# Issuing the first large load of a max-pooling kernel from SyncE instead of ScalarE

## The chip, the cores and the metric

The kernel runs on one core of a Trainium2 chip. The metric is the device time of one execution in microseconds (us); lower is better. A comparison uses the median of several executions.

## The reference

The input `x` is float32 of shape 32 x 256 x 4096 (134.2 MB) and `output_size` is 256. The reference is adaptive max pooling along the last axis:

```python
for i in range(output_size):
    start = int(i * length / output_size)
    end = int((i + 1) * length / output_size)
    result[:, :, i] = np.max(x[:, :, start:end], axis=-1)
```

4096 is a multiple of 256, so every output is the maximum of W = 16 neighbouring floats (a window, 64 bytes). There are 2,097,152 windows, 16,384 for each of the 128 partitions, and the output is 8.4 MB.

## The kernel before, in words

The windows are cut into two groups, and inside a group each partition owns one contiguous run of windows. Group A is 9,340 windows for each partition and is read by ten loads: a short one of 128 windows (8 KB in each partition), eight of 1,024 windows (64 KB in each partition, 8,192 KB in all) and one of 1,020. Group B is 7,044 windows in six loads of 1,024 and a last one of 900. The sixteen loads behind the short one are called load 0 to load 15 here, by the value of `n_loads` (load 0 is the first large one, load 8 the one of 1,020, load 15 the one of 900).

All loads go into one SBUF tile, `ring`. It has two halves of 1,176 windows (`CHUNK + GAP`). Even loads use the lower half and odd ones the upper. Every second load of a half is moved up by `GAP` = 152 windows, so two loads that follow each other in one half overlap in 872 windows only. The short load lies in the lower half at windows 1,024 to 1,151.

VectorE is the only engine that computes. `pooled` (line 56) is one `reduce_max` over windows. The short load takes one of 128 windows; every large load takes two, first the 872 windows that the next load of that half will overwrite, then the other 152. Load 15 takes a single one of 900, written back into the ring. The results lie in the tile `kept`.

Order around the change. The program order of the first three loads is: short load (line 85), load 0 (line 95), load 1 (line 95). These wait for nothing. The short load and load 1 are issued by SyncE (SP in the profile) and load 0 by ScalarE (ACT), because of the line with `queue` below. All later loads are issued by SP. Load 2 overwrites windows of load 0 and of the short load, so SP issues it only when both have landed and VectorE has reduced the short load and the first 872 windows of load 0. Load k + 2 waits for load k in the same way: for its landing and for its reduce of 872. VectorE takes its reduces in program order: the short load, then load 0, load 1 and so on.

```python
queue = nc.scalar if n_loads == 0 else nc.sync
queue.dma_start(out=ring[:, at * W : (at + n) * W], in_=xn)
...
for u, v in parts if moved else parts[::-1]:
    pooled(dst[:, u:v], at + u, v - u)
```

At the end ScalarE stores the 900 results of load 15 (line 112), and SP stores the kept results of group A and of group B (line 115).

A DMA of 128 partitions is carried by 16 DMA engines, eight partitions each; the profile counts its pieces as packets, one for each partition (8 KB for the short load, 64 KB for a large one) and one small one for each engine at the end. The profile names the two issuing queues q1 (SP) and q10 (ACT).

Of the kernel before, what the change touches and what calls it, by code (L numbers as in the profile page):

```python
# [1 line left out]

# [4 lines left out]


@with_exitstack
def kernel(  # L10
    ctx: ExitStack,
    tc: tile.TileContext,
    x: bass.AP,
    output_size: bass.AP,
    out: bass.AP,
):

    nc = tc.nc
    P = nc.NUM_PARTITIONS
    fp32 = mybir.dt.float32

    B, C, L = x.shape
    O = int(output_size)  # L30
    assert L % O == 0, (L, O)
    W = L // O
    total = B * C * O // P
    assert B * C * O % P == 0

    CHUNK = 1024
    GAP = 152
    FIRST = 128
    LOADS_A, LOADS_B = 9, 6

    LESS = 4
    group_a = [FIRST] + [CHUNK] * (LOADS_A - 1) + [CHUNK - LESS]
    last = total - sum(group_a) - LOADS_B * CHUNK
    group_b = [CHUNK] * LOADS_B + [last]
    assert 0 < last and last * (W + 1) <= CHUNK * W

    pool = ctx.enter_context(tc.tile_pool(name="pool", bufs=1))
    ring = pool.tile([P, 2 * (CHUNK + GAP) * W], fp32, tag="ring", name="ring")
    kept = pool.tile([P, total - last], fp32, tag="kept", name="kept")

    xw = x.flatten_outer_dims().rearrange("r (o w) -> (r o) w", w=W)
    ow = out.flatten_outer_dims().rearrange("r o -> (r o)")

    def pooled(dst, at, n):

        nc.vector.reduce_max(  # L56
            out=dst,
            in_=ring[:, at * W : (at + n) * W].rearrange("p (n w) -> p n w", w=W),
            axis=mybir.AxisListType.X,
        )  # L60

    taken = 0

    def group(n):

        nonlocal taken
        span = slice(taken * P, (taken + n) * P)
        taken += n
        return (
            xw[span].rearrange("(p n) w -> p (n w)", p=P),  # L70
            ow[span].rearrange("(p n) -> p n", p=P),
        )

    stores = []
    n_loads = 0
    base = 0
    for g, loads in enumerate((group_a, group_b)):
        xg, og = group(sum(loads))
        a = 0
        for n in loads:  # L80
            xn = xg[:, a * W : (a + n) * W]
            dst = kept[:, base + a : base + a + n] if n != last else None
            if n == FIRST:

                nc.sync.dma_start(
                    out=ring[:, CHUNK * W : (CHUNK + n) * W], in_=xn
                )
                pooled(dst, CHUNK, n)
            else:

                low = n_loads % 2 * (CHUNK + GAP)
                moved = n_loads // 2 % 2
                at = low + moved * GAP
                queue = nc.scalar if n_loads == 0 else nc.sync
                queue.dma_start(out=ring[:, at * W : (at + n) * W], in_=xn)
                if n != last:
                    cut = CHUNK - GAP if moved else GAP
                    parts = [(0, cut), (cut, n)]
                    for u, v in parts if moved else parts[::-1]:
                        pooled(dst[:, u:v], at + u, v - u)  # L100
                else:
                    end = (at + CHUNK) * W
                    last_kept = ring[:, end - n : end]
                    pooled(last_kept, at, n)
                n_loads += 1
            a += n
        full = a - last if g else a
        stores.append((og[:, 0:full], kept[:, base : base + full]))
        base += full
    assert taken == total  # L110

    nc.scalar.dma_start(out=og[:, full : full + last], in_=last_kept)
    tc.no_sync_barrier()
    for dst, src in stores:
        nc.sync.dma_start(out=dst, in_=src)


# [1 line left out]
_INS = ['x', 'output_size']  # L119
_OUTS = [((32, 256, 256), 'float32')]  # L120

_NUMBERS = {'output_size': 256}


# [26 lines left out]
```

## Time and profile before

| | |
|---|---|
| median of 3 executions | 337.42 us (336.9 to 337.74) |
| the profiled execution's own time | 336.9 us |
| its span | 335.1 us, 1.8 us less than its own time |
| VectorE busy | 276.3 us (82%) in 32 reduces |
| DMA | 142.61 MB, mean 426 GB/s; busy share 0.9 or near it in all 40 slices |
| reduce of 872 windows / of 152 / of 128 | 14.7 us / 2.7 us / 2.3 us |
| short load, load 0, load 1: issue to landing | 24.8, 25.0 and 43.8 us |

The span is the time from the first to the last instruction of the profiled execution; its own time is what the clock of the metric gave for that execution. Times inside the span are counted from its start. "Busy share" of DMA is the mean over the 16 DMA engines; a packet is put where it starts, so in short stretches the share can go over 1. "SPq" and "ACTq" are the queues of the issuing engines: their rows tell when a DMA was issued, not when it moved data.

### The profile page before, as it was taken

The numbers are of one execution on the slowest core, as the hardware profiler recorded it, in microseconds if no ns is written. First come the engines' busy times: TensorE is split into PE (matmuls) and PEld (weight loads), VectorE is DVE, ScalarE is ACT, GpSimd is POOL, SyncE is SP. The second block draws the span as 40 slices with busy tenths as digits, with TensorE's granted clock in tenths as the row PEclk, the third lists the DMA queues.
The fourth block names the chain that finished last, engine by engine and source line by source line (L and its number), as shares of the span: only waits on it lengthen the run. The fifth ranks groups of instructions, "written<-read, shape, count | busy, mean of one in ns | idle before, by whom it ended". The sixth has DMA issues, their size and how long they took to land.

```text
span 335.1 us, 113 instructions
## 1 busy us (share of the span) xinstructions
DVE 276.3 (82%) x32; POOL 0.2 (0%) x4
## 2 busy tenths in 40 slices
DVE  0009999698897979899797979979797997979993
POOL 0000000000000000000000000000000000000000
DMA  9998999999999999989999999999898989999997
GB/s 382 454 408 383 493 368 399 446 422 446 430 422 454 407 469 391 477 383 462 413 444 430 422 454 422 454 399 477 383 493 375 501 375 462 415 455 440 391 410 310
DMA packets 2880, 142.61 MB, mean 426 GB/s; under 512 B 320, under 2 KB 320, under 8 KB 448
## 3 DMA queue, kind: packets, MB, share of 16 engines
q1 hardware_dynamic: 2592, 133.76, 92.7%
q10 hardware_dynamic: 288, 8.85, 6.2%
HBM read 134.22 MB, written 8.39 MB: 426 GB/s over the span
## 4 chain that ended last, share of the span: by engine, by line
DMA 57%; DVE 36%; DVEq 5%; issue 0%
DMA ring<-in_x_dram 57%; DVE kept L56 36%; DVEq L146 5%
## 5 line engine op out<-in xcount | busy, mean ns | idle before, releaser
L56 DVE TENSOR_REDUCE kept<-ring 128x152 f32<-128x2432 f32 (+3 forms) x31 | 261.2, 8472 | 53.7 <-DMA ring<-in_x_dram 53.7
L56 DVE TENSOR_REDUCE ring<-ring 128x900 f32<-128x14400 f32 x1 | 15.1, 15143 | 0.0
L132 POOL MEMSET const-bfloat16-1.0<- 128x1 bf16 x1 | 0.1, 101 | 0.0
L132 POOL MEMSET const-uint8-127<- 128x1 uint8 x1 | 0.1, 101 | 0.0
L132 POOL MEMSET const-float32-0.0<- 128x1 f32 x1 | 0.1, 98 | 0.2 <-issue 0.2
L132 POOL MEMSET const-float32-1.0<- 128x1 f32 x1 | 0.1, 98 | 0.0
## 6 DMA issues: line engine op xcount, KB each, us to landing
ring<-in_x_dram SPq DMA_DIRECT2D x1, 8160.0 KB, 23.9
ring<-in_x_dram SPq DMA_DIRECT2D x1, 7200.0 KB, 21.6
out_dram<-kept SPq DMA_DIRECT2D x1, 4670.0 KB, 32.4
out_dram<-kept SPq DMA_DIRECT2D x1, 3072.0 KB, 18.2
ring<-in_x_dram SPq DMA_DIRECT2D x1, 1024.0 KB, 24.8
out_dram<-ring ACTq DMA_DIRECT2D x1, 450.0 KB, 4.2
ring<-in_x_dram SPq DMA_DIRECT2D x13, 24.0
ring<-in_x_dram ACTq DMA_DIRECT2D x1, 25.0
```

The costliest lines, as they stand in the source:

```text
L56: nc.vector.reduce_max(out=dst, in_=ring[:, at * W : (at + n) * W].rearrange("p (n w) -> p n w", w=W), axis=mybir.AxisListType.X,)
L132: nc = _bacc.Bacc("TRN2", target_bir_lowering=False, num_devices=1)
L146: with _tile.TileContext(nc) as tc:
```

## The change

Load 0 is issued by SyncE instead of ScalarE. SyncE then issues the short load, load 0 and load 1 one behind the other, all on its own queue. Sizes, places in the ring, the reduces and their order, the waits and all other DMAs stay as they are; ScalarE keeps one DMA, the store of the last 900 results.

```diff
                 low = n_loads % 2 * (CHUNK + GAP)
                 moved = n_loads // 2 % 2
                 at = low + moved * GAP
-                queue = nc.scalar if n_loads == 0 else nc.sync
-                queue.dma_start(out=ring[:, at * W : (at + n) * W], in_=xn)
+                nc.sync.dma_start(out=ring[:, at * W : (at + n) * W], in_=xn)
```

Lines behind the change move up by one: line 95 of before is line 94 after it.

## The prediction

> **What bounds the kernel now.** I read the page first: its slices, then its chain.
>
> ```profile
> DVE  0009999698897979899797979979797997979993
> DMA  9998999999999999989999999999898989999997
> ...
> DMA ring<-in_x_dram 57%; DVE kept L56 36%; DVEq L146 5%
> ```
>
> Each digit covers 8.4 us. VectorE has nothing for three slices, then pauses again and again; the DMA engines never stop. The chain alternates loads and reduces, so it doesn't yet say which of the two sets the pace. The timeline of the starts of the reduces does (start, busy time, and in brackets the idle time ahead):
>
> ```profile
> 25.58 36.67 DVE L56 TENSOR_REDUCE kept<-ring 128x128 f32<-128x2048 f32 x5 [25.58 <-DMA ring<-in_x_dram]
> 65.42 17.28 DVE L56 TENSOR_REDUCE kept<-ring 128x872 f32<-128x13952 f32 x2 [3.17 <-DMA ring<-in_x_dram]
> 84.87 17.28 DVE L56 TENSOR_REDUCE kept<-ring 128x872 f32<-128x13952 f32 x2 [2.17 <-DMA ring<-in_x_dram]
> 104.23 17.28 DVE L56 TENSOR_REDUCE kept<-ring 128x872 f32<-128x13952 f32 x2 [2.09 <-DMA ring<-in_x_dram]
> ```
>
> From 84.87 to 104.23 is 19.36 us for one load, of which VectorE needs 17.28 and waits 2.1. 8.389 MB in 19.36 us are 433 GB/s. The kernel is bound by DMA, at a constant rate; a change gains only where the DMA engines stand idle or run slowly. So I looked for such places, by cutting the span at the landings (columns: length, VectorE, GpSimd, clock, DMA share, GB/s):
>
> ```profile
> 42.48:44.96 2.48, 2.48 (x1) 0.00 (x0) 1.00 1.03 370
> 44.96:65.42 20.46, 17.29 (x4) 0.00 (x0) 1.00 0.97 416
> 65.42:84.87 19.45, 17.28 (x3) 0.00 (x0) 1.00 1.00 431
> 84.87:104.23 19.36, 17.28 (x2) 0.00 (x0) 1.00 1.00 433
> ```
>
> There is one such place before the end: load 2 takes 20.46 us after load 1, and load 3 takes 19.45, where the steady value is 19.36. That is 1.10 + 0.09 = 1.19 us lost. Why it happens is seen in the chain in order of time (start, length):
>
> ```profile
> 25.58 16.89 DVE kept L56 x2
> 42.47 0.02 issue
> 42.48 22.91 DMA ring<-in_x_dram
> ...
> 80.13 24.08 DMA ring<-in_x_dram
> ```
>
> Load 2 is issued at 42.48, and load 1, the last one in the queue, lands at 44.96: a lead of 2.48 us. Load 4 is issued at 80.13 and load 3 lands at 84.85: a lead of 4.72. A lead of 4.7 keeps the DMA engines fed, one of 2.5 doesn't. The lead is short because VectorE reduces the short load (2.29) only when load 0 has landed too: 16.89 us are 2.29 of the short load, overlapping a little, and 14.68 of load 0. And the short load comes late (24.8 us from issue to landing) because its pieces take turns with load 0's on the other queue. DMA packets from 4.9 to 24 us:
>
> ```profile
> q10 hardware_dynamic: 112, 7.34, 88.6%
> q1 hardware_dynamic: 112, 0.92, 11.3%
> ```
>
> 112 pieces of 64 KB on q10, 112 of 8 KB on q1: one for one. A piece took 0.886 x 19.1 x 16 / 112 = 2.42 us and 0.113 x 19.1 x 16 / 112 = 0.308 us. The eighth 8 KB piece of an engine thus stands behind seven of 64 KB.
>
> **The change part by part.** *Order.* On one queue the eight short pieces of an engine go ahead of load 0's. They need about 8 x 0.308 = 2.5 us, and the first ones are dearer (14 packets in the first 2.3 us):
>
> ```profile
> q1 hardware_dynamic: 14, 0.11, 32.1%
> ```
>
> 0.321 x 2.3 x 16 / 14 = 0.84 us for a cold piece, 0.54 more than a warm one. No data moves before 1.7 us, so the short load should land near 1.75 + 0.84 + 7 x 0.308 = 4.8, plus some tenths for its completion: about 5 us instead of 25.55. Its reduce of 2.29 us then lies at 5 to 7.5, under load 0's transfer, which ends some 18 us later.
>
> *Load 0.* An engine moves the same eight short and eight large pieces ahead of load 0's end; only their order differs. Load 0 lands at 25.57 as before: nothing gained, nothing lost.
>
> *Load 2.* The reduce of 872 windows starts at 25.57, not 27.78, and ends at 40.25. SP issues load 2 at 40.27 instead of 42.48, 2.21 us earlier; load 1 still lands at 44.95, so the lead is 4.68, as in the steady loop. The stretch of 1.10 and its echo of 0.09 go. What is late next: nothing but the DMA rate, 19.36 a load.
>
> *The end.* Loads 2 to 15, the reduces and the stores are chained to these landings without slack that could swallow it: load 14 lands at 297.65, then 17.07 and 15.19 of reduces, the last store and its completion. All of it moves 1.19 earlier.
>
> *Issue.* ScalarE loses one DMA (0.40 us of issue at 0.73), SP gains one. Load 0's issue moves to 1.16 behind the short load's, load 1's by about 0.43 to 1.59. Cover for load 0: 0.73 + 1.0 is where the first data of the short load moved, so load 0's pieces can start at about 2.2 to 2.8, while the short load keeps every engine busy to about 4.8. Without that cover it would cost 0.43 to 1. Load 1's pieces are wanted at 24. No wait is added; nothing is queued on SP but loads 1 and 2, which are not wanted yet. ScalarE has nothing to do until line 112.
>
> *The unknown: a cold start with short pieces only.* Before, the second piece of an engine was a large one. Its first large pieces (2.3 to 4.9 us):
>
> ```profile
> q10 hardware_dynamic: 16, 1.05, 97.3%
> ```
>
> 0.973 x 2.6 x 16 / 16 = 2.53 us, 0.11 over the warm 2.42. If only the first piece is cold, whichever follows, the change saves that 0.11. If all eight short pieces cost 0.84, it costs 7 x 0.54 = 3.8 us. I take 0, near the first end: the 8 KB pieces from 4.9 on, the nearest warm rows, take 0.308, and the pieces of 64 KB follow each other without a gap.
>
> The Trainium skill speaks against the change in one place: "DMA: Bandwidth & Descriptors", section "Issuing engines are not separate DMA queues", says that DMAs from different engines run on the same 16 DMA engines, and that issuing from several saves only the time to initiate them. By that alone the change loses an issue, 0.4 us or nothing, and gains nothing. The rows above agree on the engines and the rate; what the rule leaves out is that the queue decides who lands first. The same page's section "Measured" gives a 1 MB transfer 6.15 us (issued from GpSimd); by an estimate from that figure the short load would land at about 8 us and the sum would turn to a loss near 2 us.
>
> **The sum.** -1.19 + 0 = -1.19 us. Span 335.1 - 1.19 = 333.9; its own time 336.9 - 1.19 = 335.7. The median shown is 0.52 above that execution, so I predict 337.42 - 1.19 = 336.2 us, 0.35% less. A measurement of this kernel can tell about 0.3% (1.0 us) from no change, so the forecast stands just beyond that line.
>
> **The rivals.** *1. Real gain, too small to tell (0.32).* The lead of load 2 grows, but part of the 1.19 is given back at the start: 0.43 of a later issue, or one or two more cold pieces at 0.54 each. For it: nothing in the trace shows a single queue starting alone. Time: 336.4 + 0.43 to 1.0, so 336.5 to 337.4. That nothing changes at all also falls here: the short load's early landing seems certain, its worth isn't.
>
> *2. Slower (0.14): the cold queue of short pieces.* Place: the first 8 us, where all 16 engines have only 8 KB pieces in hand. Price: up to 3.8 us, so 337.42 - 1.19 + 3.8 = 340.0; typical, half of that, 338.1. It decides from a mean of 0.308 + (1.19 + 0.54) / 8 = 0.52 us a piece. For it: 0.84 for the cold ones, and that before, a 64 KB piece lay between any two short ones. Against it: 0.308 is already 27 GB/s an engine, the rate of the large pieces.
>
> *3. More gain (0.08).* In the start, or after, the slowest engine's lag shrinks too. The first DMA stretches show different engines starting at different times (1.7 to over 2.3 us); half a microsecond of it could go: 335.6.
>
> **How the numbers follow.** The forecast has 0.46: 336.2, within 335.8 and 336.5. With rival 3 that makes 0.54 for faster by over 0.3%, rival 1 is 0.32 within, and 0.14 slower. The range takes in the forecast, rival 3 less 0.2 for the scatter of the executions (0.4 about their median), rival 1 and the lower end of rival 2: 335.3 to 338.0.
>
> **What would show it.** Right: the first reduce starts near 5 us, alone; load 0's reduce still near 25.6; load 2's issue near 40.3, and the landings from 44.95 on all 19.36 apart; the DMA share is 1.00 from 45 to 65; span near 333.9. Wrong at the start: load 0's reduce at 26.5 or later, with a first reduce at 7 or later. Wrong on the lead: load 2 is issued 4.7 ahead and still lands 20.4 after load 1. Then the lag is that of a queue and not of the lead.

## The result and the profile after

The changed kernel takes 334.87 us (334.78 to 335.01, six executions); the kernel before took 337.50 us on the same chip (336.90 to 337.74, six executions). The ratio is 0.9925, interval 0.9913 to 0.9938: 2.6 us faster. Forecast were 336.2 us and a gain of 1.19. The direction was right; the time lies 0.4 us under the range.

The profiled execution took 334.98 us, its span is 333.2 us (before 336.9 and 335.1). Its slices:

```profile
DVE  2009979797997979799797979979797998979993
DMA  9898989899898989899898989899898989899987
```

VectorE now has something to do in the first slice. The timeline of the reduces (start, busy time, idle time ahead):

```profile
5.40 2.29 DVE L56 TENSOR_REDUCE kept<-ring 128x128 f32<-128x2048 f32 x1 [5.40 <-DMA ring<-in_x_dram]
24.75 17.28 DVE L56 TENSOR_REDUCE kept<-ring 128x872 f32<-128x13952 f32 x2 [17.07 <-DMA ring<-in_x_dram]
44.13 17.28 DVE L56 TENSOR_REDUCE kept<-ring 128x872 f32<-128x13952 f32 x2 [2.10 <-DMA ring<-in_x_dram]
63.55 17.28 DVE L56 TENSOR_REDUCE kept<-ring 128x872 f32<-128x13952 f32 x2 [2.14 <-DMA ring<-in_x_dram]
```

The short load is reduced alone at 5.40. Load 0 starts its reduce at 24.75, where before nothing was reduced until 25.58. Load 1 lands at 44.11 instead of 44.94: 0.83 us came from the start, where the forecast had nothing. The span cut at the landings shows the rest:

```profile
24.75:44.12 19.37, 17.28 (x2) 0.00 (x0) 1.00 1.00 433
44.13:63.53 19.40, 17.28 (x2) 0.00 (x0) 1.00 1.00 432
63.55:82.87 19.32, 17.28 (x2) 0.00 (x0) 1.00 1.00 434
```

The stretch of 20.46 us at load 2 is gone, and its echo. In the chain, load 2 is issued at 39.47, 4.6 us ahead of load 1's landing at 44.11:

```profile
24.75 14.70 DVE kept L56
39.45 0.02 issue
39.47 24.06 DMA ring<-in_x_dram
```

So between these two profiles 0.83 us came from the start and 1.1 from load 2 and its echo, 1.9 in all. The medians differ by 2.6: the profiled execution of before was the quickest of its six. What the others lose, and how much of it is the lead's, took experiments.

### The profile page after: what moved, and what is told of

It is laid out like the page before. It is cut to its first block, busy times and chain, and to the rows that moved or that the text cites. A ratio compares the mean times of both kernels' runs of the same rounds, so it can differ in the third digit from the quotient of the medians.

```text
span 333.2 us, 113 instructions
## 1 busy us (share of the span) xinstructions
DVE 276.5 (83%) x32; POOL 0.2 (0%) x4
## 4 chain that ended last, share of the span: by engine, by line
DMA 57%; DVE 36%; DVEq 5%; issue 0%; SPq 0%
DMA ring<-in_x_dram 57%; DVE kept L56 36%; DVEq L145 5%; SPq L85 0%
```

## The experiments

"Lead" is the time from the issue of load 2 to the landing of load 1, the last one queued ahead of it. Landing times are the last of a load's sixteen completion marks in the trace, one for each DMA engine; "spread" is from the first mark to the last. These marks, and the packet records used further down, stand in the trace; no view prints them one by one. A "lag" is what a load takes beyond the steady 19.35 us. The kernel before ran beside all of these; its medians there were 337.06, 337.60, 337.47 and 337.41 us.

**The kernel before, twice more** (b_again, b_third). No edit.

> The kernel before, unchanged, profiled a second time. Theory 1 (the gain has two terms: about 0.83 us because two queues that start at once let one DMA engine begin late, and about 1.1 us because load 2 is issued only 2.5 us ahead of load 1's landing): load 0's reduce again follows a first reduce at 25.3 us or later, and load 2 lands 20.2 to 20.7 us after load 1. Theory 2 (only the lead counts, the late landing of load 0 was an accident of that one execution): the first reduce can start anywhere from 24.7 to 25.6, and the second term is the same.

> The kernel before, profiled a third time. Two profiles of it gave load 2 at 20.45 and 21.21 us behind load 1, at the same lead of 2.5 us, and their spans differ by 0.7. If it is this lag that makes its executions differ: a span s goes with a lag of load 2 and 3 together of about s - 333.9 us (1.2 at 335.1, 1.9 at 335.8), and the landing of load 1 stays within 44.5 to 45.0.

They took 337.56 and 337.43 us; their spans are 335.8 and 335.7 us. The timeline of b_again:

```profile
25.31 36.66 DVE L56 TENSOR_REDUCE kept<-ring 128x128 f32<-128x2048 f32 x5 [25.31 <-DMA ring<-in_x_dram]
65.88 17.28 DVE L56 TENSOR_REDUCE kept<-ring 128x872 f32<-128x13952 f32 x2 [3.92 <-DMA ring<-in_x_dram]
85.44 17.28 DVE L56 TENSOR_REDUCE kept<-ring 128x872 f32<-128x13952 f32 x2 [2.28 <-DMA ring<-in_x_dram]
```

The start is late again (25.31, and 25.32 in b_third against 24.75). Load 1 lands at 44.65 in both, 0.54 later than after the change. The lead is 2.4 again, but load 2 now takes 21.21 and 21.22 us after load 1, 0.8 more than in the first profile and more than the 20.7 that was expected at most. Load 2 and load 3 together lag 2.07 and 1.88 us, close to what was expected of b_third from its span (1.8). In these three profiles what differs most is the lag of load 2; load 1's landing differs by 0.29.

**Two queues, long lead** (e1_two_long). The short load moves to a place that load 2 does not overwrite, and is reduced after load 0's 872 windows; ScalarE still issues load 0.

```diff
-                    out=ring[:, CHUNK * W : (CHUNK + n) * W], in_=xn
+                    out=ring[:, SPOT * W : (SPOT + n) * W], in_=xn   # SPOT = CHUNK + GAP + CHUNK
...
+                            with tc.issue_after(first):   # load 0's 872
+                                late = pooled(*short)
...
```

> The kernel before with both queues at the start, but a long lead: the short load lies in the upper half of the ring and is reduced after the 872 windows of load 0. Theory 1: the start stays late (first reduce near 25.5 us), load 2 is issued near 40.3 and lands 19.4 us after load 1, so only the lead's term goes: 337.5 - 1.1 = 336.4 us. Theory 2 (only the lead): 334.9 us, as the changed kernel.

Measured: 335.45 us (335.25 to 335.50), ratio 0.9948 (0.9935 to 0.9960). The start is late and load 2 no longer is:

```profile
25.38 36.66 DVE L56 TENSOR_REDUCE kept<-ring 128x872 f32<-128x13952 f32 x5 [25.38 <-DMA ring<-in_x_dram]
63.91 17.28 DVE L56 TENSOR_REDUCE kept<-ring 128x872 f32<-128x13952 f32 x2 [1.88 <-DMA ring<-in_x_dram]
```

Load 1 lands at 44.54, and with a lead of 4.45 load 2 lands 19.34 behind it. The lead alone brings 1.6 us, more than the 1.1 expected, and without touching the queue. What is left to the changed kernel, some 0.4 to 0.6 us, is the late start.

**One queue, load 0 ahead of the short load** (e2_one_short).

```diff
+                if n_loads == 0:   # behind load 0's dma_start, on nc.sync
+                    xs, ds, ns = short
+                    nc.sync.dma_start(
+                        out=ring[:, CHUNK * W : (CHUNK + ns) * W], in_=xs
+                    )
+                    pooled(ds, CHUNK, ns)
```

> One queue (SP) for everything, as changed, but the short load is issued behind load 0, so that it lands with it and its 2.3 us of reduce delay load 2 again (lead about 2.4 us). Theory 1: load 0 and the short load land at 24.7 us or a little earlier, load 2 lands about 20.4 us after load 1: 334.9 + 1.1 = 336.0 us. If the lag of load 2 belongs to two queues and not to the lead: 334.9 us. If only the lead counts (theory 2): 337.5 us.

Measured: 335.44 us (335.30 to 335.68), ratio 0.9950 (0.9937 to 0.9964). This missed its aim: load 0 landed 2.5 us before the short load, VectorE took its 872 windows first, from 22.96, load 2 was issued at 39.86 and the lead was 4.9, not 2.4. There was no lag (19.34). But it shows something else: load 1 lands at 44.76, 0.65 us later than after the change, with one queue. The first packets in flight (window 0 to 2.35 us):

```profile
q1 hardware_dynamic: 16, 1.05, 135.9%
```

1.359 x 2.35 us = 3.2 us for each of the sixteen first pieces of 64 KB, against 2.42 in the steady loop. The spread of load 1's marks is 0.86 us, against 0.33 after the change. A late start doesn't need a second queue.

**A small DMA on the second queue** (e3_tiny_act), added to the changed kernel.

```diff
+                nc.scalar.dma_start(out=tiny[:, :], in_=xn[:, 0:W])
                 nc.sync.dma_start(
```

> The changed kernel plus one small DMA on ScalarE's queue at the start (64 bytes for each partition, 8 KB in all, its result unused), issued together with the short load. Theory 1 in its narrow form (two queues that are handed work in the same instant make an engine begin late, whatever the size): the short load's reduce starts near 6 us and load 0's near 25.5; 334.9 + 0.8 = 335.7 us. If it is the large pieces between the short ones that delay the start (theory 3): 334.9 to 335.1 us, load 0's reduce at 24.8.

Measured: 335.02 us (334.95 to 335.47), load 0's reduce at 24.88:

```profile
5.54 2.29 DVE L56 TENSOR_REDUCE kept<-ring 128x128 f32<-128x2048 f32 x1 [5.54 <-DMA ring<-in_x_dram]
24.88 17.28 DVE L56 TENSOR_REDUCE kept<-ring 128x872 f32<-128x13952 f32 x2 [17.05 <-DMA ring<-in_x_dram]
```

Two queues that start together cost some 0.1 us here. The narrow form of theory 1 falls.

**Two queues with small first pieces** (e7_two_small). SP issues the short load; ScalarE issues load 0, cut into 8 KB and 56 KB for each partition, and load 1.

```diff
-                nc.sync.dma_start(out=ring[:, at * W : (at + n) * W], in_=xn)
+                queue = nc.scalar if n_loads < 2 else nc.sync
+                for u, v in ((0, 128), (128, n)) if n_loads == 0 else ((0, n),):
+                    queue.dma_start(...)
```

> Two queues at the start, but only 8 KB pieces first: SP issues the short load, ScalarE issues load 0 in two DMAs (8 KB and 56 KB for each partition) and load 1 behind them. The lead is long. If large pieces among the first ones cause the late start (theory 3): load 1 lands at 44.2 or earlier, 334.9 to 335.2 us. If two queues do it (theory 1): load 1 lands at 44.5 to 44.9, 335.5 us or more.

Measured: 338.37 us, scattered from 335.86 to 339.60, and no answer on its question. The profile is of one of the quick executions (336.06). In it load 0 landed at 25.08, 0.35 later than after the change, between the two theories. Then load 2 on SP's queue took turns with the rest of load 1 on ScalarE's, so that load 1 landed at 46.85 only, load 3 was issued 2.2 us ahead of load 2's landing, and a short lead was back one load later.

**The price of the lead on one queue.** The changed kernel, with some windows of load 0 reduced once more ahead of its 872, into a place that is overwritten later (in e4 into a tile of its own). The order of the reduces behind it is fixed to that of the changed kernel.

```diff
+                    if n_loads == 0:
+                        first = pooled(spare, at + cut, EXTRA)   # EXTRA = 64, 128, 192 or 256
...
```

> The changed kernel once more, as the control for the three runs beside it: 334.9 us, load 0's reduce at 24.8, a lead of 4.6 us (issue of load 2 to the landing of load 1), load 2's reduce 19.4 us after load 1's.

> The changed kernel, with 64 windows of load 0 reduced once more ahead of its 872 (1.2 us of VectorE, result unused), so that load 2 is issued that much later: lead 3.5 us. If the lag of load 2 is a matter of the lead alone: a small loss, 0 to 0.4 us, 334.9 to 335.3. If it needs two queues at the start: 334.9 us.

> The changed kernel, with 128 windows of load 0 reduced once more ahead of its 872 (2.2 us of VectorE, result overwritten later): lead 2.4 us as in the kernel before, but on one queue. With 64 windows (lead 3.5) load 2 took 19.66 us. If the lead decides: load 2 lands 20.3 to 21.2 us after load 1, 1.0 to 2.0 us lost, 336.0 to 337.0 us. If a lag at this lead needs two queues at the start: under 335.4 us.

> The changed kernel with 192 windows reduced once more: lead about 1.35 us, between 2.42 (no lag) and 0.40 (2.0 us lag). If on one queue each us of lead below 2.4 costs one: load 2 lands 20.3 to 20.6 us after load 1, time 335.9 to 336.2 us.

> The same with 256 windows (4.3 us): lead about 0.3 us. If the lead decides and each us below about 3.5 costs one us: load 2 lands 22.5 to 23.5 us after load 1, 338.1 to 339.1 us. A loss much under 3 us would mean that something makes it good later.

| kernel | lead, us | load 2 behind load 1, us | time, us |
|---|---|---|---|
| a_again (no extra windows) | 4.6 | 19.33 | 335.15 (334.80 to 335.38) |
| e4_lead_64 | 3.5 | 19.66 | 335.04 (334.97 to 335.37) |
| e5b_lead_128 | 2.4 | 19.39 | 335.01 (334.81 to 335.11) |
| e8_lead_192 | 1.5 | 21.41 | 336.63 (336.05 to 337.12) |
| e6b_lead_256 | 0.4 | 21.35 | 337.07 (336.82 to 338.12) |

Of e5b's two branches the second came, and the theory that the lead alone decides falls: 2.4 us of lead cost the kernel before 1.2 to 2.1 us in its profiles, and cost nothing here. The 0.3 us that load 2 lags in e4 doesn't show in its times. Nor is the price a slope. From 2.4 to 1.5 the lag jumps to about 2 us (the median rises by 1.6, more than was expected of e8), and from 1.5 to 0.4 it grows no more (e6b was expected at 338.1 or more). The windows at the joint between load 1 and load 2 (length, VectorE, GpSimd, clock, DMA share, GB/s) show this. In e5b_lead_128 there is no gap:

```profile
42.50:44.50 2.00, 2.00 (x2) 0.00 (x0) 1.00 1.23 524
44.50:46.50 2.00, 2.00 (x1) 0.00 (x0) 1.00 1.21 524
```

In e6b_lead_256 no piece starts for 2 us, and in the kernel before (the last pair) fewer do:

```profile
42.50:44.50 2.00, 2.00 (x2) 0.00 (x0) 1.00 0.00 0
44.50:46.50 2.00, 2.00 (x2) 0.00 (x0) 1.00 1.55 524
```

```profile
42.50:44.50 2.00, 2.00 (x1) 0.00 (x0) 1.00 0.84 295
44.50:46.50 2.00, 2.00 (x2) 0.00 (x0) 1.00 0.70 262
```

**What differs at the same lead.** The kernel before has two queues and unequal engines (spread of load 1's marks 0.8 to 1.0 us); e5b has one queue and a spread of 0.3. Two kernels were to separate these: e10_skew_lead is e2 with 144 windows reduced once more (one queue, unequal engines), e9_tiny_lead_128 is e3 with 128 (two queues, nearly equal engines). The edits are those shown for e2, e3 and the extra windows; in e10 the order of the reduces is fixed to the extra windows, load 0's 872, the short load.

> One queue with load 0 ahead of the short load (as e2, whose engines end load 1 over 0.86 us instead of 0.33) and 144 windows reduced once more: lead 2.4 us. If unequal engines make the lag: load 2 lands 20.3 to 21.3 us after load 1, 335.4 + 1.0 to 2.0 = 336.4 to 337.4 us. If it takes a second queue: 335.4 to 335.6 us.

> The changed kernel with the small DMA on ScalarE's queue at the start (as e3) and 128 windows reduced once more: lead 2.4 us, both queues used, engines nearly equal. If the use of the second queue makes the lag: 336 to 337 us. If unequal engines make it: 334.9 to 335.3 us.

e10: 337.54 us, load 2 lands 21.52 us behind load 1. So one queue is enough for the lag. But of its twelve executions four took 335.27 to 335.41 and eight 337.01 to 338.28, with none between. e9: 337.57 us; three executions took 335.28 to 335.99, nine 337.32 to 338.96. Its expectation gave that time to the second queue: against e5b only the tiny DMA is added, the spread of load 1's marks is nearly as small (0.42 against 0.31) and the lead is 2.5. The windows and the timeline of e9_tiny_lead_128, in its slowest execution:

```profile
42.50:44.50 2.00, 2.00 (x2) 0.00 (x0) 1.00 1.01 426
```

```profile
24.77 36.74 DVE L56 TENSOR_REDUCE kept<-ring 128x128 f32<-128x2048 f32 x5 [17.07 <-DMA ring<-in_x_dram]
66.20 17.28 DVE L56 TENSOR_REDUCE kept<-ring 128x872 f32<-128x13952 f32 x2 [4.68 <-DMA ring<-in_x_dram]
```

At the joint 426 GB/s are in place of 524. In the packet records, load 2 is issued at 41.68. Thirteen engines begin it between 43.47 and 43.87, straight behind load 1. The other three begin at 45.1, 45.6 and 46.0, that is 3.4 to 4.3 us after the issue, the first of them with a piece of 3.32 us where 2.42 is usual. Load 2's marks run from 63.78 to 66.17, thirteen of them to 64.17. The load has landed when its last engine has, so three engines of sixteen make 2.0 of the 2.6 us of lag. The rest falls on all: the pieces begun beside the late ones mostly took 2.8 to 3.1 us instead of 2.42.

The lag, then, is made of a pause of some or all engines between load 1 and load 2, and of slow pieces behind it. e6b shows both on every engine: all had ended load 1 by 43.84, load 2 was issued at 43.73, its first pieces began between 44.69 and 45.16 and took 2.79 to 3.45 us. In b_again eight engines began load 2 between 1.4 and 2.0 us after its issue and eight between 2.4 and 3.2.

Which engines pause isn't explained. That those pause which run out before load 2's pieces come is a natural guess, but in e9 the five engines that ended load 1 first (43.46 to 43.52) went straight on, and the three that paused ended it between 43.55 and 43.77. (The records don't name the engine; each end is matched with the start right behind it.) Nor are unequal engines shown to be a cause of their own: from the issue to the first engine's end of load 1 it is 1.0 to 1.2 us in e10 and the kernel before, and 1.8 us in e5b and e9. So e10 differs from e5b in that time too, and between e5b and e9, where it is the same, the second queue is the one difference: none of six executions lost time, and nine of twelve lost over 2 us.

At a lead of 2.4 the same kernel can do both. The kernel before shows the two groups as well: of the 31 executions beside these runs, five took 335.19 to 335.51 and 25 took 336.68 to 338.16 (one 339.96). The lower group equals e1, which has the same start and no lag.

**Two queues, a lead between** (e11_two_mid): e1 with 64 windows reduced once more.

> As e1 (both queues at the start, short load out of the way) with 64 windows reduced once more: lead about 3.3 us. The kernel before loses 1.2 to 2.0 us at 2.5, e1 nothing at 4.5. If the loss grows evenly as the lead falls below some 3.5 to 4: 0.2 to 1.0 us, 335.7 to 336.5 us. If it is the one-queue rule (nothing above 2.4): 335.4 us.

Measured: 336.30 us, from 335.32 to 337.62, with a lead of 3.3. In the profiled execution load 2 has no lag (19.36), but load 3 lands 20.34 us behind load 2, by one engine: its other fifteen had landed at 83.17, the last did at 84.35. VectorE was still late by the extra windows, so that lead was 3.3 too. But the packet records show no pause there: that engine went straight on to load 3 at 63.59, and its first piece took 3.51 us instead of 2.42. So a time within the expected range doesn't confirm a loss that grows with a shorter lead, and why that piece was slow is open.

## Why the prediction was wrong in size

*Order: right.* The short load landed at 5.37 and was reduced alone at 5.40 (forecast 4.8 plus some tenths). Moving it ahead of load 0's pieces cost load 0 nothing.

*Load 2: the right mechanism, mis-sized.* The issue came at 39.47 (forecast 40.27; the reduce began 0.83 earlier), the lead was 4.64 (forecast 4.68), and the stretches behind it are 19.32 to 19.40 as forecast. But the term was put at 1.19 us from the one profile of before. Two more profiles of it show 2.07 and 1.88 (load 2 and load 3 together, over 19.35 each), the two groups of its executions lie about 2 us apart, and load 2 lags by 2.0 to 2.1 in e8 and e6b. The first failed step is to size a wait that differs between executions from one execution, and the quickest one shown: the offset of 0.52 between that execution and the median was carried over as if it were scatter, and it was part of the term. That a lead of 2.5 doesn't keep the engines fed holds for the kernel before and not in general: e5b lost nothing at 2.4.

*Load 0: wrong, the second failed step.* "Nothing gained, nothing lost" missed 0.83 us in that profile and 0.5 to 0.6 against b_again and b_third (load 1's landing); e1 puts it at 0.4 to 0.6 us of the time. The count of pieces was right, and so is their mean: the mean of load 1's sixteen marks is 44.11 before and 43.95 after. What changed is the spread, 1.03 us before and 0.33 after, and the last engine decides: before, fifteen of the marks lay by 44.26 and the last at 44.94. The prediction's baseline was off as well: load 0 landed at 25.73 before (25.0 after its issue at 0.73) and at 24.73 after; 25.57 is the short load. Rival 3 named a shrinking lag of the slowest engine, with a chance of 0.08. That large pieces among the first ones are sufficient for it is shown by e2. Whether the second queue adds its own part isn't settled: e3 says at most 0.1 us for tiny pieces, e7 has 0.35 with 8 KB pieces on both.

*The unknown at the start: the end taken was right.* Pieces of 8 KB behind one another weren't cold for long; rival 2 didn't come. In the first 2.35 us the changed kernel's sixteen first pieces took 0.312 x 2.35 = 0.73 us each, and the 108 pieces of the next 2.25 us 0.960 x 2.25 x 16 / 108 = 0.32:

```profile
q1 hardware_dynamic: 16, 0.13, 31.2%
...
q1 hardware_dynamic: 108, 0.88, 96.0%
```

The estimate from the Trainium skill's 6.15 us for 1 MB issued from GpSimd ("DMA: Bandwidth & Descriptors", section "Measured") would have put the short load's landing near 8 us; it was 5.37.

*Issue and end: right.* The 0.4 us of issue stayed hidden, and all later loads, reduces and stores moved with load 2: load 14's reduce starts at 295.75 instead of 297.67. The rule that issuing engines share the same DMA engines (same page, section "Issuing engines are not separate DMA queues") holds for the rate, 433 GB/s before and after; here the choice of queue was worth 2.6 us through the order of landing and the evenness of the start.

*Two bounds don't follow from their terms.* Rival 1's 336.4 plus 0.43 to 1.0 begins at 336.8, not 336.5; rival 3's 335.6 less 0.2 is 335.4, not 335.3. The time lies below either.

With the measured sizes the sum closes: 2.0 for the lag, as in b_again and b_third, and 0.5 to 0.6 for the start are 2.5 to 2.6 of the 2.63 us.

## What to carry to other kernels

This DMA-bound loop lost time at a joint, where one load ended and the next had only just been issued. In such a loop, list the time from each issue to the moment the queue ahead of it runs out, and widen the smallest, above all where a small transfer that is wanted first shares the engines with large ones of another queue. Here a lead of 4.4 us or more never showed a lag at load 2, and one of 2.4 did in some executions and not in others; so read several profiles, or several times, before pricing such a lead. And begin a stream with small pieces: the spread of load 1's marks was 0.2 to 0.55 us in the kernels whose first pieces were all small, and 0.6 to 1.0 where 64 KB pieces were among the first two, and the last engine sets every landing.

## What the runs showed of the hardware that was not expected

- Engines that pause between two loads take the next one up at very different times: 1.0 to 1.4 us after its issue in e6b, where all sixteen had run out; up to 3.2 us in b_again and 3.4 to 4.3 us in e9, where others were at work. Their first pieces are slow as well, 2.79 to 3.45 us in e6b instead of 2.42. Why is open.
- An unevenness between the engines that arises in the first 3 us can last: in e2 the marks of load 1 are 0.86 us apart, and those of load 14 still 0.85. Larger ones shrank (in e9 from 2.62 us at load 4 to 1.26 at load 14), but the landings stayed 19.3 to 19.5 us apart meanwhile, so no lag was made good.
- A load can lag with a long lead: in e9, load 4 took 20.60 us after load 3 although its lead to the last mark was 4.6 us. Load 3's first engines had ended 2.4 us before its last, and three first pieces of load 4 took 4.1 to 4.2 us; that the one comes of the other isn't shown.
